# Stick-breaking attention: the clamp ahead of the softplus logarithm on GpSimd in place of VectorE

## The chip, the cores and the metric

The kernel runs on one core of one Trainium2 chip. The metric is the device time of one execution in microseconds; the time before is the median of three runs. An execution has five engines that run side by side, each through its own queue in order: TensorE (PE, with its weight loads as PEld), VectorE (DVE), ScalarE (ACT), GpSimd (POOL) and SyncE (SP), which only issues DMAs here.

## The reference

A trunk of two layers over 512 tokens of width 1024, all in float32: layer 0 mixes with an mLSTM, layer 1 with stick-breaking attention; after each mixer come a cross-attention into 256 memory tokens and a SwiGLU feed-forward of width 2816. The change lies in the mixer of layer 1, 16 heads of width 64:

```python
z = jnp.einsum('bhtd,bhsd->bhts', qb, kb) * scale
strict = s_idx < t_idx
log_1m = jnp.where(strict, jax.nn.log_sigmoid(-z), 0.0)
suffix = lax.cumsum(log_1m, axis=3, reverse=True) - log_1m
a = jnp.where(strict, jnp.exp(jax.nn.log_sigmoid(z) + suffix), 0.0)
outs.append(jnp.einsum('bhts,bhsd->bhtd', a, vb))
```

log_sigmoid(-z) is minus the softplus of z, so every score goes through one softplus, and the suffix sums and the final exponential follow from it.

## The kernel before

Every operation is first recorded in a plan, with an engine, a planned duration and the tiles that it reads and writes; `lay_out` then gives each engine its order by a list scheduling with due times (TensorE's recorded order sets the due times, tiles wait for free slots: 8 banks of PSUM, 44 "big" and 8 "half" buffers), and `emit` writes the instructions in the order of their planned starts. A planned duration that changes therefore moves other work. Some copies have an alternative engine: `copy` may go to ScalarE or, when VectorE is planned to be free earlier, to VectorE (L454 to L457).

Products are made from split operands (a high and a low part in float32r), three matmuls for one product. `split` (L546) makes the high part with a copy (L455 on ScalarE, L456 on VectorE) and the low part with a subtraction on VectorE (L470).

`stick` (L1216) works through 8 pairs of heads. For each pair `open_pair` (L1308) makes five banks of scores of 128x512 (zc, two zb, two za): matmuls of keys and queries (`scores`), closed by one matmul with the mask. Each bank goes through `softplus` (L1291): exp on ScalarE from the bank into a buffer s, the minimum with 1e13 on s, the logarithm of 1 + s on ScalarE, the maximum of z and s on VectorE, which reads the bank, and the split. Then `subtract` lets TensorE subtract the suffix sums from the same five banks, `weights` takes the exponentials, and the products with v follow. While a pair's softplus chains run, TensorE works on projections of the next pairs, on v, and on the keys of the cross-attention (`between`, the table STICK at L60).

So for each bank there is a stretch between its last score matmul and its first subtract matmul, which TensorE fills with a projection, and in which the five-step chain of softplus has to end. GpSimd's queue holds, in this stage, memsets of the key and query tiles (L503, two to a pair) and DMAs of the residual rows and the gains (L432). All five engines run in order, so that an instruction which waits holds back what is queued behind it on its engine.

Of the kernel before, what the change touches and what calls it, by code (L numbers as in the profile page):

```python
# [14 lines left out]
ALU = mybir.AluOpType  # L15
# [60 lines left out]
class View:  # L76
# [41 lines left out]
    def ap(self):  # L118
        r = self.buf.tile
        for s in self.steps:  # L120
            if isinstance(s, tuple):
                r = r[s]
            elif isinstance(s, int):
                r = r.rearrange("p (m n) -> p m n", n=s)
            elif s == "two":
                r = r.rearrange("p (a m) n -> p a m n", a=2)
            else:
                r = r.bitcast(s)
        return r
# [262 lines left out]
class Trunk:  # L392
# [823 lines left out]
    def stick(self, h, w_qkv, w_out, filler, finish):  # L1216
# [73 lines left out]

        def softplus(z, s, t):  # L1291
            self.act(s, z, AF.Exp)
            self.ts(s, s, 1e13, None, ALU.min)
            self.act(s, s, AF.Ln, bias=1.0)
            self.tt(s, z, s, ALU.max)
            self.split(t, s)
# [11 lines left out]
        def open_pair(qk):  # L1308

            zc, zb, za = self.bank(NT, P), {}, {}  # L1310
            scores(zc, zc[:, 0::2], [(e, 2, zc[:, 2 * e : 2 * e + 2]) for e in range(2)], qk)

            s, c = self.half(NT, P), Pair(self.big(6, P, dt=R), self.big(6, P, dt=R))
            softplus(zc, s, c[:, 0:4])
            sb, b = self.big(2, NT, P), Pair(self.big(2, NT, P, dt=R), self.big(2, NT, P, dt=R))
            for e in range(2):
                zb[e] = self.bank(NT, P)
                scores(zb[e], zb[e][:, 0::3], [(e, 1, zb[e][:, 0:3]), (e, 3, zb[e][:, 3:4])], qk)
                softplus(zb[e], sb[:, e], b[:, e])
            u = s[:, 1::2]  # L1320
            self.tt(u, u, sb[:, :, 3], ALU.add)
            self.split(c[:, 4:6], u)

            self.tt(sb[:, :, 1:3], sb[:, :, 1:3], s.pairs(), ALU.add)
            x = Pair(self.big(2, 3, P, dt=R), self.big(2, 3, P, dt=R))
            self.split(x, sb[:, :, 0:3])
            a = {}
            for e in range(2):
                za[e] = self.bank(NT, P)
                scores(za[e], za[e][:, 0], [(e, 0, za[e])], qk)  # L1330
                t = self.big(2, NT, P, dt=R)
                a[e] = Pair(t[:, 0], t[:, 1])
                softplus(za[e], self.half(NT, P), a[e])
            return zc, zb, za, c, b, a, x
# [410 lines left out]
```

## Time and profile before

| | us |
|---|---|
| median of three runs (1484.99 to 1488.79) | 1485.59 |
| the profiled execution, its own time | 1486.58 |
| span of its profile, first to last instruction | 1484.9 |
| TensorE busy | 1469.4 (99%) |
| VectorE busy | 1197.8 (81%) |
| ScalarE busy | 865.8 (58%) |
| GpSimd busy | 143.6 (10%) |
| the eight pairs of the stage with the change | from about 770 to 945 |

The mean granted clock of TensorE is 0.997 of its higher level. A busy share is a mean over all stages; the matmuls are pipelined and their ends are modelled, so that a matmul's duration is longer than the distance to the next one's start. Starts are therefore what to read of TensorE, and the same holds in a small measure for VectorE and ScalarE, where a row's start lies some 0.08 us ahead of the end of the row before it. Groups of rows are named by the line of the helper that recorded them (L470 is any two-operand VectorE operation, L475 any VectorE operation with scalars).

### The profile page before, as it was taken

To read this page: it belongs to the slowest core of one execution; us is meant where nothing else is said; L and a number is where in the kernel's file an instruction comes from. 1 tells how busy PE (TensorE), PEld (TensorE's weight loads), DVE (VectorE), ACT (ScalarE), POOL (GpSimd) and SP (SyncE) were. 2 spreads that over 40 slices of the span, in tenths; PEclk is the share of its full clock that TensorE was granted. 3 is DMA by queue.
4 is the path that set the end of the run, shared out by engine and by line. 5 is a ranking of instruction groups with operands and counts; after the bars stand their busy time and mean duration, and the time that the engine had idled before them with its cause. 6 is when DMAs were issued, how large, how long until landed. Compare 5 with 4: busy or idle time off the path is not lost.

```text
span 1484.9 us, 26101 instructions
## 1 busy us (share of the span) xinstructions
PE 1469.4 (99%) x10335; PEld 1370.6 (92%) x10335; DVE 1197.8 (81%) x1851; ACT 865.8 (58%) x1495; POOL 143.6 (10%) x179
## 2 busy tenths in 40 slices
PE   9999899999999999999999999999999999999998
PEld 7999889998999999998889889888988999999996
DVE  7988879887787877897838998878787968778985
ACT  7768656564654554544538997766546644444632
POOL 3100100100011111110100001001000111110100
PEclk9999999999999999999999999999999999999999
DMA  8445646532655575675343459255414563854741
GB/s 224 90 100 143 199 135 206 108 121 85 174 110 128 96 161 129 137 189 162 110 113 93 99 164 254 102 174 126 140 63 132 119 142 72 213 114 100 152 161 57
DMA packets 173228, 200.43 MB, mean 135 GB/s; under 512 B 8241, under 2 KB 142129, under 8 KB 173106
## 3 DMA queue, kind: packets, MB, share of 16 engines
q1 hardware_dynamic: 126192, 131.65, 28.8%
q0 software_dynamic: 46912, 67.12, 23.3%
q8 instruction: 81, 1.33, 0.4%
q14 instruction: 41, 0.34, 0.1%
q10 hardware_dynamic: 2, 0.00, 0.0%
HBM read 176.20 MB, written 10.49 MB: 126 GB/s over the span
## 4 chain that ended last, share of the span: by engine, by line
PE 94%; DMA 2%; DVE 2%; ACT 1%; issue 1%; DVEq 0%; POOL 0%; POOLq 0%; ACTq 0%
PE ps L526 92%; PE ps L540 2%; DMA big<-in_ffn_w_down_dram 1%; DVE big L470 1%; DMA big<-in_ml_w_in_dram 1%; ACT big L455 0%; DVE big L482 0%; ACT half L448 0%; DMA big<-in_norm_gains_dram 0%; DVE sm L475 0%; DVE half L470 0%; DVE sm L482 0%; ACT sm L448 0%; DVE big L456 0%; ACT half L455 0%
## 5 line engine op out<-in xcount | busy, mean ns | idle before, releaser
L526 PE MATMUL ps<-big,big 128*128 128x256 f32 (+2 forms) x9762 | 1407.4, 305 | 5.8 <-ACT big L455 2.8
L526 PEld LDWEIGHTS ps<-big,big 128*128 128x128 f32 (+1 forms) x9762 | 1298.0, 188 | 91.1 <-ACT big L455 3.3
L470 DVE TENSOR_TENSOR big<-big,big 128x1024 fp32r<-128x1024 f32 (+2 forms) x541 | 626.4, 1191 | 45.7 <-ACT big L455 25.1
L455 ACT CAST big<-big 128x1024 fp32r<-128x1024 f32 (+1 forms) x422 | 417.6, 1021 | 162.2 <-DMA big<-in_ffn_w_gate_up_dram 45.2
L470 DVE TENSOR_TENSOR big<-ps,big 128x512 fp32r<-128x512 f32 (+3 forms) x197 | 114.4, 605 | 44.2 <-ACT big L455 31.5
L455 ACT COPY half<-ps 128x512 f32<-128x512 f32 (+1 forms) x112 | 65.5, 585 | 124.1 <-PE ps L526 116.4
L455 ACT CAST big<-ps 128x512 fp32r<-128x512 f32 (+1 forms) x159 | 76.9, 513 | 99.6 <-PE ps L526 64.8
L448 ACT ACTIVATE half<-ps 128x512 f32<-128x512 f32 (+2 forms) x137 | 79.4, 581 | 90.2 <-PE ps L526 84.6
L448 ACT ACTIVATE half<-big 128x512 bf16<-128x512 f32 (+2 forms) x64 | 42.1, 659 | 73.0 <-DVE big L470 45.9
L437 POOL DMA_DIRECT2D big<-in_ffn_w_gate_up_dram x40 | 51.1, 1278 | 316.9 <-DVE big L470 217.4
L470 DVE TENSOR_TENSOR big<-half,big 128x512 fp32r<-128x512 f32 (+4 forms) x126 | 76.6, 625 | 5.9 <-ACT big L448 3.3
L482 DVE SCALAR_TENSOR_TENSOR half<-ps,half 128x512 f32<-128x512 f32 (+3 forms) x74 | 47.0, 645 | 36.4 <-PE ps L526 18.0
L455 ACT CAST big<-half 128x512 fp32r<-128x512 f32 (+3 forms) x82 | 43.9, 558 | 10.7 <-DVE half L470 6.3
L470 DVE TENSOR_TENSOR half<-ps,half 128x512 f32<-128x512 f32 (+1 forms) x54 | 36.4, 687 | 15.4 <-PE ps L526 11.9
L448 ACT ACTIVATE big<-ps 128x512 fp32r<-128x512 f32 (+2 forms) x66 | 39.6, 612 | 15.2 <-PE ps L526 11.8
L470 DVE TENSOR_TENSOR big<-ps,gain 128x512 f32<-128x512 f32 x32 | 22.0, 687 | 31.8 <-ACT half L448 30.0
L540 PE MATMUL ps<-const,big 128*128 128x128 f32 (+1 forms) x314 | 41.9, 270 | 0.8 <-DVE big L482 0.8
L540 PEld LDWEIGHTS ps<-const,big 128*128 128x128 f32 (+1 forms) x314 | 36.0, 140 | 6.0 <-DVE big L482 1.1
L475 DVE TENSOR_SCALAR sm<-sm,sm 128x1 f32<-128x1 f32 x101 | 24.2, 243 | 20.2 <-ACT half L448 11.4
L448 ACT ACTIVATE half<-half 128x512 f32<-128x512 f32 (+1 forms) x50 | 30.8, 630 | 10.3 <-DVE half L470 10.2
L482 DVE SCALAR_TENSOR_TENSOR big<-big,sm,gain 128x512 f32<-128x512 f32 (+1 forms) x45 | 34.9, 808 | 0.6
L482 DVE SCALAR_TENSOR_TENSOR big<-big,sm,big 128x512 f32<-128x512 f32 (+1 forms) x49 | 34.1, 737 | 0.8
(92 smaller groups left out, 588.2 us busy)
## 6 DMA issues: line engine op xcount, KB each, us to landing
big<-in_ffn_w_gate_up_dram SPq DMA_DIRECT2D x68, 512.0 KB, 5.0
big<-in_ffn_w_gate_up_dram POOLq DMA_DIRECT2D x40, 512.0 KB, 6.1
big<-in_ffn_w_down_dram SPq DMA_DIRECT2D x36, 512.0 KB, 5.9
big<-in_xa_w_kv_dram SPq DMA_DIRECT2D x32, 512.0 KB, 5.4
big<-in_sb_w_qkv_dram SPq DMA_DIRECT2D x24, 512.0 KB, 4.1
big<-big SPq DMA_DIRECT2D x80, 128.0 KB, 2.3
big<-in_ml_w_in_dram SPq DMA_DIRECT2D x18, 512.0 KB, 5.3
dr<-big POOLq DMA_DIRECT2D x16, 512.0 KB, 4.2
```

The lines of the kernel that those rows point to most:

```text
L437: "POOL", 1040, lambda nc: nc.gpsimd.dma_start(ap(out), ap(in_), accum_op=ALU.add), [in_, out], [out], load=ns
L448: nc.scalar.activation(ap(out), ap(in_), func, scale=ap(scale), **kw)
L455: "ACT", 0.833 * n + (60 if psum else 95), lambda nc: nc.scalar.copy(ap(out), ap(in_)), [in_], [out],
L470: self._dve(out, [a, b], lambda nc: getattr(nc, q).tensor_tensor(out=ap(out), in0=ap(a), in1=ap(b), op=op), eng)
L475: nc.vector.tensor_scalar(out=ap(out), in0=ap(a), scalar1=ap(s1), scalar2=ap(s2), op0=op0, **kw)
L482: lambda nc: nc.vector.scalar_tensor_tensor(out=ap(out), in0=ap(a), scalar=ap(s), in1=ap(b), op0=op0, op1=op1),
L526: nc.tensor.matmul(ap(out), lhsT=ap(a), rhs=ap(b), start=start, stop=stop, **kw)
L540: nc.tensor.transpose(ap(out), ap(in_), ap(ident))
```

## The change

One line of `softplus`. The minimum is recorded for GpSimd, with a planned duration of 700 ns, where `ts` recorded it for VectorE with 66 + 0.52 x 512 = 332 ns:

```diff
         def softplus(z, s, t):
             self.act(s, z, AF.Exp)
-            self.ts(s, s, 1e13, None, ALU.min)
+            self.plan.op("POOL", 700, lambda nc: nc.gpsimd.tensor_scalar(out=ap(s), in0=ap(s), scalar1=1e13, scalar2=None, op0=ALU.min), [s], [s])
             self.act(s, s, AF.Ln, bias=1.0)
             self.tt(s, z, s, ALU.max)
             self.split(t, s)
```

Forty instructions change their engine, five in each pair. Since the plan sees other durations, the orders of all engines change between the first and the last pair and are the same ahead of it and behind it. VectorE loses 40 instructions and takes 16 more copies than before (nine more casts of 128x1024 and seven more of 128x512, and one plain copy more against one cast of 128x256 less); ScalarE has 16 fewer. TensorE's instructions are the same in number and kind. In pairs 1 to 5 their order is the same too; in pairs 0, 6 and 7 the first subtract comes three matmuls earlier.

TensorE in pair 0, before: the end of the projection (the tile ps_8907, three matmuls to one product) and the first subtract, on the bank ps_8863. The numbers behind names are running numbers that differ between the two kernels.

```order
L526 MATMUL ps_8907<-big_8338,big_8707 128x512
L526 MATMUL ps_8907<-big_8373,big_8701 128x512
L526 MATMUL ps_8907<-big_8338,big_8701 128x512
L526 MATMUL ps_8863<-big_8930,const_459 128x512
L526 MATMUL ps_8863<-big_8919,const_459 128x512
L526 MATMUL ps_8863<-big_8939,const_459 128x2x128
L526 MATMUL ps_8863<-big_8932,const_459 128x2x128
L526 MATMUL ps_8969<-big_8316,big_8810 128x512
```

The same place after; the projection's tile is ps_8911 here:

```order
L526 MATMUL ps_8863<-big_8939,const_459 128x512
L526 MATMUL ps_8863<-big_8929,const_459 128x512
L526 MATMUL ps_8863<-big_8946,const_459 128x2x128
L526 MATMUL ps_8863<-big_8935,const_459 128x2x128
L526 MATMUL ps_8911<-big_8338,big_8707 128x512
L526 MATMUL ps_8911<-big_8373,big_8701 128x512
L526 MATMUL ps_8911<-big_8338,big_8701 128x512
L526 MATMUL ps_8970<-big_8316,big_8810 128x512
```

The last three matmuls of the projection stood ahead of the four subtracts and now stand behind them.

VectorE in pair 0, before, from the last evacuation of a projection to the first low part: the three minima, and the maxima of the first three banks.

```order
L482 SCALAR_TENSOR_TENSOR big_8869<-ps_8826,big_8869 128x512
L475 TENSOR_SCALAR half_8877<-half_8877 128x512
L475 TENSOR_SCALAR big_8889<-big_8889 128x512 x2
L470 TENSOR_TENSOR half_8877<-ps_8863,half_8877 128x512
L470 TENSOR_TENSOR big_8889<-ps_8871,big_8889 128x512
L470 TENSOR_TENSOR big_8889<-ps_8882,big_8889 128x512
L470 TENSOR_TENSOR big_8930<-half_8877,big_8919 128x512
L475 TENSOR_SCALAR half_8925<-half_8925 128x512
```

After:

```order
L482 SCALAR_TENSOR_TENSOR big_8869<-ps_8826,big_8869 128x512
L456 CAST big_8892<-big_8850 128x1024
L470 TENSOR_TENSOR big_8901<-big_8850,big_8892 128x1024
L470 TENSOR_TENSOR half_8877<-ps_8863,half_8877 128x512
L470 TENSOR_TENSOR big_8890<-ps_8871,big_8890 128x512
L470 TENSOR_TENSOR big_8890<-ps_8882,big_8890 128x512
L456 CAST big_8935<-big_8890 128x512
L470 TENSOR_TENSOR big_8939<-half_8877,big_8929 128x512
L470 TENSOR_TENSOR big_8946<-big_8890,big_8935 128x512 x2
```

The minima are gone; a split of a weight (the cast and the subtraction of 128x1024) stands in their place ahead of the maxima, and one cast of 128x512 that ScalarE made stands ahead of the low parts.

GpSimd in pair 7, after; before, these four DMAs of residual rows stood in a row with nothing between them:

```order
L1293 TENSOR_SCALAR half_10655<-half_10655 128x512
L1293 TENSOR_SCALAR big_10664<-big_10664 128x512
L432 DMA big_10685<-dr_8270 128x1024
L432 DMA big_10702<-dr_8364 128x1024
L1293 TENSOR_SCALAR big_10664<-big_10664 128x512
L1293 TENSOR_SCALAR half_10711<-half_10711 128x512
L432 DMA big_10737<-dr_8506 128x1024
L1293 TENSOR_SCALAR half_10739<-half_10739 128x512
L432 DMA big_10766<-dr_8565 128x1024
```

The minima of the third, fourth and fifth bank are queued behind DMAs.

## Rows read from the trace of the kernel before

**Rows 1.** The longest of TensorE's waits over the whole span, of six that the view lists (who waited for whom: us in total, times, longest us), and the stretch of the chain that ended last which covers the stage (start us, us, what).

```profile
PE ps L526 <- ACT big L455: 2.8, 1, 2.8
...
739.95 220.16 PE ps L526 x1222
```

**Rows 2.** Busy time by stretch, from 780 to 940 us (us; PE, PEld, DVE, ACT and POOL busy with counts, granted clock, DMA share, GB/s): one stretch of 20 us and the sum of the eight.

```profile
840.00:860.00 20.00, 20.00 (x104) 17.20 (x103) 18.56 (x31) 18.31 (x34) 3.44 (x6) 1.00 0.59 160
...
sum 160.00, PE 160.00 PEld 142.37 DVE 145.39 ACT 139.17 POOL 9.82; mean PE 20.00 PEld 17.80 DVE 18.17 ACT 17.40 POOL 1.23
```

**Rows 3.** The minima, by their line, from 760 to 945 us (durations min/median/max in ns), and one of VectorE's groups by shape from 780 to 940 us (count | busy us, mean ns | idle before).

```profile
L475 DVE TENSOR_SCALAR half<-half x24: 416/423/429, 772.8 to 932.8; 128x512 f32<-128x512 f32 x24
L475 DVE TENSOR_SCALAR big<-big x16: 415/428/553, 773.4 to 927.5; 128x512 f32<-128x512 f32 x16
...
L456 DVE CAST big<-big 128x1024 fp32r<-128x1024 f32 x1 | 0.7, 689 | 0.0
```

**Rows 4.** GpSimd's timeline near the start of the program: the four selects, which read and write their tile in place, as the minimum does (start us, us).

```profile
23.89 1.20 POOL L508 TENSOR_SCALAR_AFFINE_SELECT half<-half 128x512 f32<-128x512 f32 x1
25.00 0.68 POOL L508 TENSOR_SCALAR_AFFINE_SELECT half<-half 128x512 f32<-128x512 f32 x1
25.59 0.44 POOL L508 TENSOR_SCALAR_AFFINE_SELECT half<-half 128x256 f32<-128x256 f32 x1
25.95 1.66 POOL L508 TENSOR_SCALAR_AFFINE_SELECT half<-half 128x512 f32<-128x512 f32 x1
```

**Rows 5.** VectorE's timeline over the same time (start us, us).

```profile
21.75 0.16 DVE L482 SCALAR_TENSOR_TENSOR sm<-sm,sm 128x1 f32<-128x1 f32 x1
...
23.33 1.22 DVE L470 TENSOR_TENSOR big<-big,big 128x1024 fp32r<-128x1024 f32 x1
24.46 0.69 DVE L470 TENSOR_TENSOR big<-ps,big 128x512 fp32r<-128x512 f32 x1
25.07 0.63 DVE L482 SCALAR_TENSOR_TENSOR sm<-sm,sm 128x1 f32<-128x1 f32 x1
25.62 1.50 DVE L470 TENSOR_TENSOR big<-big,big 128x1024 fp32r<-128x1024 f32 x1
```

**Rows 6.** VectorE's timeline in pair 0 (start us, us, and in brackets the idle time before it and its releaser).

```profile
772.76 0.42 DVE L475 TENSOR_SCALAR half<-half 128x512 f32<-128x512 f32 x1
...
775.26 1.28 DVE L470 TENSOR_TENSOR big<-ps,big 128x512 f32<-128x512 f32 x2
776.45 0.68 DVE L470 TENSOR_TENSOR big<-half,big 128x512 fp32r<-128x512 f32 x1
777.05 0.42 DVE L475 TENSOR_SCALAR half<-half 128x512 f32<-128x512 f32 x1
777.39 0.69 DVE L470 TENSOR_TENSOR big<-big,big 128x512 fp32r<-128x512 f32 x1
...
778.66 0.69 DVE L470 TENSOR_TENSOR big<-big,big 128x512 fp32r<-128x512 f32 x1
```

**Rows 7.** TensorE's timeline in pairs 0, 6 and 7: the first subtract of the pair (four matmuls, big<-const as the matrix of the suffix sums is constant), and in pair 7 the filling projection ahead of it.

```profile
780.00 0.86 PE L526 MATMUL ps<-big,const 128*128 128x512 f32 x4
...
909.02 0.86 PE L526 MATMUL ps<-big,const 128*128 128x512 f32 x4
...
929.75 5.18 PE L526 MATMUL ps<-big,big 128*128 128x256 f32 x42
934.76 0.86 PE L526 MATMUL ps<-big,const 128*128 128x512 f32 x4
```

**Rows 8.** VectorE's timeline in pairs 6 and 7: in pair 6 the first minimum and the third bank's maximum, and in both the low parts that the first subtract needs last.

```profile
902.01 0.43 DVE L475 TENSOR_SCALAR half<-half 128x512 f32<-128x512 f32 x1
...
904.86 0.68 DVE L470 TENSOR_TENSOR big<-ps,big 128x512 f32<-128x512 f32 x1
...
907.67 0.69 DVE L470 TENSOR_TENSOR big<-big,big 128x512 fp32r<-128x512 f32 x1
...
933.18 1.29 DVE L470 TENSOR_TENSOR big<-big,big 128x512 fp32r<-128x512 f32 x2
```

**Rows 9.** Pair 3: ScalarE's exp of the second bank and its logarithms of the fourth and fifth, VectorE's low parts of the two zb banks, and VectorE's rows behind the subtracts, with their idle times.

```profile
835.29 0.60 ACT L448 ACTIVATE half<-ps 128x512 f32<-128x512 f32 x1
...
839.02 1.15 ACT L448 ACTIVATE half<-half 128x512 f32<-128x512 f32 x2
...
842.04 1.29 DVE L470 TENSOR_TENSOR big<-big,big 128x512 fp32r<-128x512 f32 x2
...
848.97 0.69 DVE L482 SCALAR_TENSOR_TENSOR big<-ps,big 128x512 fp32r<-128x512 f32 x1 [0.38 <-ACT big L448]
849.58 0.68 DVE L470 TENSOR_TENSOR big<-half,big 128x512 fp32r<-128x512 f32 x1
850.43 0.69 DVE L470 TENSOR_TENSOR big<-half,big 128x512 fp32r<-128x512 f32 x1 [0.18 <-ACT big L448]
851.41 0.69 DVE L470 TENSOR_TENSOR big<-half,big 128x512 fp32r<-128x512 f32 x1 [0.29 <-ACT big L448]
```

**Rows 10.** TensorE's timeline in pair 3: the filling projection, the first subtract, and the first product with v.

```profile
836.86 9.98 PE L526 MATMUL ps<-big,big 128*128 128x512 f32 x42
846.68 0.86 PE L526 MATMUL ps<-big,const 128*128 128x512 f32 x4
...
851.12 2.12 PE L526 MATMUL ps<-big,big 128*128 128x256 f32 x11
```

## The prediction

> **What bounds the kernel now.** I read first who ended the span. The chain of waits shows one single piece from 739.95 us on, 220.16 us of TensorE's matmuls, 1222 of them with no other engine between [rows 1]. The whole stage with the change (770 to 945 us) lies in it. Next the list of TensorE's waits: the longest of the six in the whole program is 2.8 us, and none lies in this stage, since the chain would show it [rows 1]. Matmul durations overlap, so I check by starts: the 42 filling matmuls of 128x512 in pair 3 take 846.68 - 836.86 = 9.82 us, 0.234 us each, with nothing lost between them [rows 10]. So TensorE is the bound, and it is fed without a gap. Taking work off VectorE can then gain nothing directly; the change can only cost, by delaying what TensorE takes up. How near that is, the stretches show: from 780 to 940 us VectorE is busy 145.39 of 160 us and ScalarE 139.17, GpSimd 9.82 [rows 2]. VectorE has 14.6 us of idle time, 9%.
>
> **What leaves VectorE.** Forty minima at a median of 423 to 428 ns [rows 3]. The next instruction starts 0.34 us after one (777.05 to 777.39) [rows 6], so VectorE is freed of 40 x 0.34 = 13.6 us, all beside busy matmuls: worth 0 on the path. The plan gives 16 copies to VectorE instead: nine of 128x1024, whose one example takes 689 ns [rows 3], less 0.08 us of overlap about 0.6 each, and seven of 128x512, of the minimum's size and duration, about 0.34: 5.4 + 2.4 = 7.8 us. ScalarE is freed of them; it was not the bound, 0 on the path. TensorE keeps all its matmuls, 0.
>
> **What a minimum costs on GpSimd.** The trace has none there. The nearest rows are the selects of 128x512 near the start, which also read and write one tile in place. They show 1.20, 0.68 and 1.66 us [rows 4], and the spread has a cause that VectorE's rows show [rows 5]. The first, from 23.89, ends at 25.10, 0.55 after a VectorE operation with two operands in SBUF has ended (23.33 + 1.22 = 24.55). The last ends at 27.61, 0.49 after such an operation (25.62 + 1.50 = 27.12). The second meets an operation with an operand in PSUM (24.46) and takes 0.68. In turn VectorE is held: a 128x1 operation that takes 0.16 us at 21.75 takes 0.63 at 25.07 and ends with the second select, and the subtraction at 25.62 takes 1.50 for 1.22, since the select of 128x256 ends at 26.03. So in this trace a GpSimd operation that reads SBUF and a VectorE operation with two SBUF operands go one after the other. I take 0.55 us for the minimum itself, with bounds of 0.49 and 1.66, plus the time for which it waits or makes VectorE wait.
>
> The Trainium skill has this rule and it speaks against the change (SBUF — State Buffer, Who interferes with whom): GpSimd has only the second port pair of VectorE, and one holder locks the other out for a whole instruction, also when VectorE merely reads two operands from SBUF. The rows at 25.07 and 25.62 agree. Without the rule the sum below would be 0; by it at its full length it becomes the first rival.
>
> **Pairs 1 to 5** keep TensorE's order, with 9.8 us of filler in pair 3. There VectorE writes the low parts for the first subtract until 842.04 + 1.29 = 843.33 [rows 9], and TensorE takes them at 846.68 [rows 10]: 3.35 us to spare. The four later minima, 2.2 us of GpSimd, run beside a cast, a subtraction of 128x1024 and a cast of 128x512, 0.6 + 1.2 + 0.34 = 2.1 us. One after the other from 835.89, the end of the second exp, they end at 840.2; the fifth logarithm now starts at about 839.5 (two in 1.15 from 839.02) [rows 9]. The chain is 0.7 us late, against 3.35, and behind the subtracts VectorE idles for 0.38, 0.18 and 0.29 us [rows 9], which takes the lateness up. Cost 0, at most 0.4 for each pair: 0 to 2.0.
>
> **Pair 0.** Three matmuls fewer stand ahead of the first subtract, so TensorE reaches it 3 x 0.234 = 0.70 us earlier, at 779.30 for 780.00 [rows 7]; the third matmul, the first that needs the last low part, at 779.77. That part now ends at 778.66 + 0.69 = 779.35 [rows 6]. The new order takes out two minima ahead of it and the sum of 128x256, and puts a cast in: 0.65 us less, 778.70, if nothing is held. That is 1.07 us to spare. Held one after the other: from 772.76 [rows 6], when the first minimum is ready, three minima, a cast and a subtraction of 128x1024 share VectorE's second operand, 3 x 0.55 + 0.6 + 1.2 = 3.45 us, to 776.2. The third logarithm follows (0.1 + 0.62), then the maximum (0.69): 777.6, where it now ends at 775.26 + 1.28 = 776.54. So 1.1 us late: 779.8. The fourth and fifth minimum may hold the three low parts for 0.55 each: 779.8 to 780.9 against 779.77. TensorE loses 0 to 1.1 us; I take 0.6.
>
> **Pair 6.** The same three matmuls are taken from ahead of the first subtract, so its third matmul comes at 909.02 + 0.46 - 0.70 = 908.78 [rows 7]. Ahead of the maxima stand only a cast and a subtraction of 128x512, so the shared time is 3 x 0.55 + 0.34 + 0.60 = 2.6 us from 902.01; the third maximum ends at about 906.0, for 905.54 now [rows 8], 0.5 late. The last low part, 907.67 + 0.69 = 908.36 now, is 0.65 earlier by the order: 908.2, and up to 1.1 more. Loss 0 to 0.5, taken 0.2.
>
> **Pair 7.** The three matmuls are of 128x256, (934.76 - 929.75) / 42 = 0.119 us each [rows 7]: the third subtract at 935.22 - 0.36 = 934.86. The low parts end at 933.18 + 1.29 = 934.47 [rows 8], 0.68 earlier without two minima, 933.8. Three minima are queued on GpSimd behind DMAs, and two of VectorE's subtractions of 128x1024 run beside the first ones. One of these can hold a minimum for 1.2 us, and each minimum a low part for 0.55: up to 2 us late, loss 0 to 1.0, taken 0.5. Behind such a minimum only DMAs wait, for rows that are wanted after the output projection: 0.
>
> **The sum.** 0.6 + 0.2 + 0.5 = 1.3 us, bounds 0 and 1.1 + 0.5 + 1.0 + 2.0 = 4.6. Against the profiled execution 1486.58 + 1.3 = 1487.9; that one lies 1.0 above the median of the three runs, so against the median 1485.59 + 1.3 = 1486.9.
>
> **Rivals.** *VectorE becomes the bound of the pairs by being held.* Each minimum holds VectorE for its full 0.55 us: 22.0 us, plus 7.8 of copies, less 13.6: 16.2 against 14.6 us of idle time. Per pair VectorE comes 5 x 0.55 = 2.75 us late to the rows behind the subtracts; idle time there gives back 0.85. The first product with v takes its operand at 851.12, which VectorE ends at 849.58 + 0.68 = 850.26 [rows 9, 10]: 0.86 to spare. So 1.0 us is lost in each of eight pairs, 8 us: 1493.9. It decides once a pair's lateness passes 1.7 us. For it: 9% of idle time is little, and more than half of VectorE's work here has two SBUF operands. Against it: the five maxima read PSUM, and much of a minimum can run beside them.
>
> *The minimum is slow on GpSimd in itself*, at the upper bound of 1.66 us. In pair 0 three take until 777.7, the third maximum ends at 779.2, and a cast and three low parts later it is 781.4 against 779.77: 1.6 lost, also in pairs 6 and 7. In pair 3 four take from 835.89 to 842.5, the fifth maximum is some 2.4 late, and behind 0.86 and 0.85 us of slack 0.7 is lost. 3 x 1.6 + 5 x 0.7 = 8.3, and 15 at 2 us for each: 1494 to 1501. For it only that no row shows this operation; against it the ends at 0.49 and 0.55.
>
> *Relief of VectorE pays*: for faster by 0.3%, 4.5 us would have to come out of TensorE's stage, which shows no wait. Something would have to shorten matmuls: 1481.
>
> **How the numbers follow.** About 0.3%, 4.5 us, is what a measurement of this kernel can tell from no change. Forecast, 1485.5 to 1490: 0.66. VectorE held: 0.23. Slow minimum: 0.08. Relief pays: 0.03. The forecast's bounds lie within 0.3% but for its last tenth; so faster 0.03, same 0.66, slower 0.31. The range takes in the forecast, a little below for the spread of the runs (1484.99 was seen), and the first rival with 1 us on top: 1484.8 to 1495.0; outside stay the slow minimum and the relief, 0.11, and the edges.
>
> **What would show it.** Right: forty rows of the changed line on GpSimd near 0.55 us, longer where a two-operand row of VectorE is under way, VectorE's low parts longer than 0.69 beside them; TensorE's order of time without a gap in pairs 1 to 5 and gaps of under 1.1 us ahead of the first subtracts of pairs 0, 6 and 7. The first rival: gaps ahead of the products with v in every pair. The second: rows of over 1.2 us on GpSimd with VectorE at its maxima. Wrong altogether: a gap of several us in one place, such as a minimum behind a DMA whose tile is not free.

## The result, and the profile after

The kernel after takes 1502.35 us (median of five runs, 1500.98 to 1503.06), the one before on the same chip 1485.52 (five runs, 1484.99 to 1488.79): the ratio is 1.0109, 95% interval 1.0095 to 1.0123. That is 16.8 us slower, where 1.3 were predicted, and outside the predicted range. The profiled execution took 1500.98 us and has a span of 1499.3 us, for 1486.58 and 1484.9 before.

The page of after begins with the busy times of the engines (us, share of the span, instructions); the row on the minimum is from its list of the costliest groups (count | busy us, mean ns | idle time of GpSimd before them).

```profile
PE 1474.5 (98%) x10335; PEld 1372.3 (92%) x10335; DVE 1198.3 (80%) x1827; ACT 857.0 (57%) x1479; POOL 208.3 (14%) x219
...
L1293 POOL TENSOR_SCALAR half<-half 128x512 f32<-128x512 f32 x24 | 37.9, 1579 | 96.4 <-ACT half L448 88.7
```

The view by source line shows the forty minima (durations min/median/max in ns), and who waited for them (us, times).

```profile
L1293 POOL TENSOR_SCALAR half<-half x24: 1479/1488/2030, 770.4 to 947.1; 128x512 f32<-128x512 f32 x24
L1293 POOL TENSOR_SCALAR big<-big x16: 1481/1488/2166, 772.2 to 943.3; 128x512 f32<-128x512 f32 x16
...
  ACT half L448: 14.6, 16
  ACT big L448: 10.3, 12
```

A minimum takes 1.49 us, three and a half times the 0.42 that it took on VectorE [rows 3], and up to 2.17 where something holds it. Five of them are needed for each pair.

TensorE's list of waits (us in total, times, longest us), of which the longest was one of 2.8 us ahead of the stage [rows 1], now begins with this:

```profile
PE ps L526 <- DVE big L470: 11.8, 17, 1.6
```

What is late there, the chain of waits shows in pair 1 (start us, us, what; the short pieces between them are left out).

```profile
794.45 0.60 ACT half L448
...
795.20 1.49 POOL half L1293
...
796.77 1.49 POOL big L1293
...
798.34 1.49 POOL big L1293
...
799.90 1.49 POOL half L1293
...
801.47 1.50 POOL half L1293
...
802.99 0.64 ACT half L448
...
803.65 0.57 DVE half L470
```

ScalarE's exponential releases the first minimum; from there the five stand one behind the other at a pitch of 1.57 us, the fifth logarithm follows at 802.99, the fifth maximum at 803.65, and the low parts behind them. VectorE's timeline over the same time shows what that does to its queue (start us, us, idle time before and its releaser):

```profile
798.96 0.69 DVE L470 TENSOR_TENSOR big<-ps,big 128x512 f32<-128x512 f32 x1
800.52 0.69 DVE L470 TENSOR_TENSOR big<-ps,big 128x512 f32<-128x512 f32 x1 [0.88 <-ACT big L448]
802.09 0.69 DVE L470 TENSOR_TENSOR half<-ps,half 128x512 f32<-128x512 f32 x1 [0.87 <-ACT half L448]
803.65 0.69 DVE L470 TENSOR_TENSOR half<-ps,half 128x512 f32<-128x512 f32 x1 [0.88 <-ACT half L448]
...
806.40 0.42 DVE L470 TENSOR_TENSOR big<-ps,big 128x256 fp32r<-128x256 f32 x1
```

VectorE waits some 0.87 us ahead of each of the last three maxima, and what is queued behind them waits too. The last row is such work: it evacuates a bank of the filling projection, whose matmuls of 128x256 then take the bank anew. TensorE's timeline shows who needs it, and the first subtracts of pairs 0 and 6, where [rows 7] have no wait:

```profile
778.56 0.73 PE L526 MATMUL ps<-big,const 128*128 128x512 f32 x2 [1.54 <-DVE big L470]
780.17 0.79 PE L526 MATMUL ps<-big,const 128*128 128x256 f32 x2 [0.89 <-DVE big L470]
...
806.87 2.03 PE L526 MATMUL ps<-big,big 128*128 128x256 f32 x15 [1.45 <-DVE big L470]
...
917.21 0.74 PE L526 MATMUL ps<-big,const 128*128 128x512 f32 x2 [0.75 <-DVE big L470]
918.83 0.51 PE L526 MATMUL ps<-big,const 128*128 128x256 f32 x2 [0.88 <-DVE big L470]
```

Behind the waits of pairs 0 and 6 TensorE's clock is at its lower level for a while, which the stretches show (us; busy times of PE, PEld, DVE, ACT, POOL; granted clock; DMA share; GB/s):

```profile
778.00:780.00 2.00, 0.73 (x2) 0.30 (x2) 2.00 (x3) 1.07 (x2) 1.92 (x2) 0.90 0.00 0
780.00:782.00 2.00, 1.82 (x5) 1.58 (x6) 1.97 (x5) 1.52 (x3) 1.49 (x3) 0.50 0.00 0
782.00:784.00 2.00, 2.00 (x8) 1.58 (x7) 2.00 (x4) 2.00 (x5) 0.00 (x0) 0.74 0.01 4
...
920.00:923.00 3.00, 3.00 (x14) 2.90 (x14) 3.00 (x6) 3.00 (x7) 0.29 (x1) 0.50 0.93 307
```

0.50 is 1.2 GHz for 2.4. Behind pair 0's waits TensorE loses some (0.10 + 0.50 + 0.26) x 2 = 1.7 us by it, behind pair 6's about as much (an estimate from these rows).

**Where the 16 us lie.** TensorE has the same matmuls in both kernels, so the start of the same matmul can be set side by side. Pair by pair the kernel after falls behind by 4.2, 1.7, 0.7, 1.6, 1.6, 0.5, 3.7 and 2.4 us, 16.4 in the stage; ahead of it there are two jumps, one near 680 us, together 2.4 us the other way, in a part where the two programs are the same; behind it the distance stays at 14.0 to 14.7 us, which is the distance of the two profiled executions. The eleven waits that the timeline shows in pairs 0 to 6 and the two of pair 7 come to 10.1 us, the lower clock to about 3.4. Of the rest, 2.9, some 2.1 is the first 0.2 us or so of each wait, which the modelled end of the matmul before it covers: from start to start the thirteen waits come to 12.2. About 0.8 stays open.

### The profile page after: what moved, and what is told of

The parts are those of the page before. It is cut to its first block, busy times and chain, and to the rows that moved or that the text cites. A ratio compares the mean times of both kernels' runs of the same rounds, so it can differ in the third digit from the quotient of the medians.

```text
span 1499.3 us, 26119 instructions
## 1 busy us (share of the span) xinstructions
PE 1474.5 (98%) x10335; PEld 1372.3 (92%) x10335; DVE 1198.3 (80%) x1827; ACT 857.0 (57%) x1479; POOL 208.3 (14%) x219
## 4 chain that ended last, share of the span: by engine, by line
PE 89%; DVE 3%; POOL 3%; ACT 3%; DMA 2%; issue 1%; SPq 0%; DVEq 0%; POOLq 0%; ACTq 0%
PE ps L526 86%; PE ps L540 2%; DVE big L470 2%; POOL half L1293 2%; ACT big L455 2%; DMA big<-in_ml_w_in_dram 1%; POOL big L1293 1%; ACT half L448 1%; DVE big L482 0%; DMA big<-big 0%; ACT big L448 0%; DVE half L470 0%; ACT half L455 0%; DVE big L456 0%; SPq L432 0%
## 5 line engine op out<-in xcount | busy, mean ns | idle before, releaser
L470 DVE TENSOR_TENSOR big<-big,big 128x1024 fp32r<-128x1024 f32 (+3 forms) x541 | 628.9, 1195 | 41.6 <-ACT big L455 20.8
L455 ACT CAST big<-big 128x1024 fp32r<-128x1024 f32 (+1 forms) x406 | 405.1, 1028 | 162.1 <-DMA big<-in_ffn_w_gate_up_dram 46.9
L1293 POOL TENSOR_SCALAR half<-half 128x512 f32<-128x512 f32 x24 | 37.9, 1579 | 96.4 <-ACT half L448 88.7
L526 PE MATMUL ps<-big,const 128*128 128x512 f32 (+2 forms) x160 | 35.7, 358 | 7.9 <-DVE big L470 7.9
L432 POOL DMA_DIRECT2D dr<-big x16 | 8.7, 544 | 240.3 <-DVE sm L475 213.5
```

Of the source, the lines that this page charges most:

```text
L432: self.plan.op(eng, cost, lambda nc: getattr(nc, q).dma_start(ap(out), ap(in_)), [in_, *behind], [out], load=ns)
L455: "ACT", 0.833 * n + (60 if psum else 95), lambda nc: nc.scalar.copy(ap(out), ap(in_)), [in_], [out],
L470: self._dve(out, [a, b], lambda nc: getattr(nc, q).tensor_tensor(out=ap(out), in0=ap(a), in1=ap(b), op=op), eng)
L526: nc.tensor.matmul(ap(out), lhsT=ap(a), rhs=ap(b), start=start, stop=stop, **kw)
L1293: self.plan.op("POOL", 700, lambda nc: nc.gpsimd.tensor_scalar(out=ap(s), in0=ap(s), scalar1=1e13, scalar2=None, op0=ALU.min), [s], [s])
```

## The experiments

**Order or duration?** The first kernel keeps the instruction order of after on every engine and cuts the minimum to 16 of the 512 columns; the second cuts it to 256. The rest of s is left unclamped.

```diff
-            self.plan.op("POOL", 700, ... out=ap(s), in0=ap(s) ..., [s], [s])
+            part = s[:, 0:1, 0:16]          # the second kernel: s[:, 0:2]
+            self.plan.op("POOL", 700, ... out=ap(part), in0=ap(part) ..., [s], [s])
```

> The order of every engine is that of the changed kernel, but each of the forty GpSimd minima covers 16 of the 512 columns (the other scores go unclamped). Length theory (a minimum takes 1.49 us on GpSimd, five stand in a row in each pair, and the softplus chains end too late for the first subtract) and hold theory (VectorE's operations with two operands in SBUF wait for GpSimd's reads): the cause is gone with the length, so 1485 to 1488 us. Order theory (the order that the plan laid out for 700 ns is worse in itself, with three matmuls less ahead of the first subtracts of pairs 0, 6 and 7): still 1498 to 1502.

Measured: 1486.7 us (ten runs) against 1485.62 of before on the same chip, ratio 1.0005 (0.9996 to 1.0015). No wait of TensorE is left in the stage, and its matmuls keep their distance to those of the kernel before to within 0.1 us from the first pair to the last. The durations:

```profile
L1294 POOL TENSOR_SCALAR half<-half x24: 237/247/1437, 772.9 to 932.0; 128x16 f32<-128x16 f32 x24
```

So the new order of all engines, the casts that went to VectorE and the three matmuls that moved cost nothing that this trace shows, and at most 2.2 us by the interval. The order by itself is not the cause.

> Same order again, each minimum over 256 of the 512 columns (the other half goes unclamped). If the 1.49 us go by columns, each takes about 0.75, near the planned 0.70. Length theory: the chains end when the plan meant them to, 1485.5 to 1489 us. Hold theory: half of the held time is left, so about half of the loss, 1492 to 1495. Order theory: 1498 to 1502.

Measured: 1489.05 us, ratio 1.0023 (1.0013 to 1.0032); one wait of TensorE in pair 0.

```profile
L1294 POOL TENSOR_SCALAR half<-half x24: 839/850/1722, 772.5 to 934.2; 128x256 f32<-128x256 f32 x24
```

With the same order the time goes from 1486.7 over 1489.05 to 1502.35 us as the median duration goes from 0.25 over 0.85 to 1.49. The loss isn't in proportion: 0.6 us more cost 2.4, the next 0.64 cost 13.3. That slack takes up most of the first step is the likely reason, not one that a run singles out.

**Lateness or held ports?** In the third kernel three memsets of s stand in place of each minimum: about the same time on GpSimd in the same order, but nothing is read. The attention then works on constants.

```diff
-            self.plan.op("POOL", 700, ... out=ap(s), in0=ap(s) ..., [s], [s])
+            def three(nc):
+                for _ in range(3):
+                    nc.gpsimd.memset(ap(s), 1.0)
+
+            self.plan.op("POOL", 700, three, [s], [s])
```

> Each minimum is replaced with three memsets of the same tile, which only write (the scores are lost, all of the attention works on constants); at about 0.45 us from one to the next they fill GpSimd for about as long as the minimum did, in the same place of the chain and the same order. Length theory: the loss stays, 1499 to 1503 us. Hold theory: VectorE isn't held by an operation that reads nothing, so the loss goes, 1486 to 1490.

Measured: 1505.4 us (four runs), ratio 1.0136 (1.0120 to 1.0152). Three memsets take 1.70 us from the start of the first to the end of the third (median), 0.2 more than a minimum. The memsets, and VectorE's subtractions of two SBUF operands beside them (count | busy us, mean ns | idle before):

```profile
L1295 POOL MEMSET half<- x72: 520/526/1104, 773.0 to 953.6; 128x512 f32 x72
```

```profile
L470 DVE TENSOR_TENSOR big<-big,big 128x1024 fp32r<-128x1024 f32 x14 | 17.0, 1221 | 0.2
...
L470 DVE TENSOR_TENSOR big<-big,big 128x512 fp32r<-128x512 f32 x20 | 13.1, 683 | 0.1
```

In the kernel before, over the same stretch (780 to 940 us):

```profile
L470 DVE TENSOR_TENSOR big<-big,big 128x1024 fp32r<-128x1024 f32 x18 | 21.6, 1219 | 0.0
...
L470 DVE TENSOR_TENSOR big<-big,big 128x512 fp32r<-128x512 f32 x20 | 13.2, 687 | 0.0
```

So VectorE isn't held here, and the loss is there in full and 3 us on top, with operations that are 0.2 us longer. In the kernel after the subtractions take longer, so VectorE is held there, but a loss of this size doesn't need it; what the hold adds in the kernel after, this run doesn't tell:

```profile
L470 DVE TENSOR_TENSOR big<-big,big 128x1024 fp32r<-128x1024 f32 x17 | 21.6, 1285 | 0.2
...
L470 DVE TENSOR_TENSOR big<-big,big 128x512 fp32r<-128x512 f32 x19 | 13.4, 729 | 0.1
```

**The plan's price.** The plan of after counts 700 ns for a minimum. This kernel gives it 1570, its pitch in pair 1, and lets the plan order everything anew.

```diff
-            self.plan.op("POOL", 700, ...
+            self.plan.op("POOL", 1570, ...
```

> The changed kernel with the minimum planned at 1570 ns, the distance from one to the next in its trace, so that the order is laid out for it: two matmuls of a filling projection of some 0.23 us more for each 0.5 us ahead of the first subtracts of pairs 0 and 6 (9.2 us of filler for 7.1). Length theory: most of the loss of pairs 0, 6 and 7 goes (some 10 of 16 us), that of pairs 1 to 5, whose TensorE order stays, remains: 1489 to 1495 us. Hold theory: the held time is the same, 1497 to 1503.

Measured: 1490.93 us (five runs), ratio 1.0036 (1.0023 to 1.0049). 16.8 us become 5.3: two thirds of the loss go when the order is made for the duration that the minimum has. In pair 0, 30 filling matmuls of 128x512 now stand ahead of the first subtract, where the order of after has 21:

```profile
772.22 7.16 PE L526 MATMUL ps<-big,big 128*128 128x512 f32 x30
...
780.61 0.51 PE L526 MATMUL ps<-big,const 128*128 128x256 f32 x2 [0.78 <-DVE big L470]
```

The wait of 2.43 us in that place shrinks to 0.78. One of the waits left is new (TensorE's list of waits, of the whole program):

```profile
PE ps L526 <- DVE big L470: 2.4, 5, 0.9
PE ps L526 <- DMA big<-big: 2.0, 1, 2.0
```

By TensorE's starts against the kernel before, 3.8 of the 6.0 us that this kernel loses in the stage lie at that one stop at 926.90 us, the wait and the lower clock behind it (0.72 from 925 to 930 us). The late softplus chains are left with some 2.

**Without a minimum.** The line is taken out; s is unclamped.

> No minimum at all (the scores go unclamped into the logarithm), laid out anew: what the relief of VectorE by 13.6 us is worth by itself. TensorE is the bound and waits for nothing in the stage, so 1484.5 to 1486.5 us; if relief of VectorE were worth something here, 1480 to 1483.

Measured: 1484.49 us (eleven runs) against 1486.75, ratio 0.9990 (0.9981 to 0.9998). That is all that the relief of VectorE is worth in the order that the plan makes for it, with no work on GpSimd either; in the stage itself TensorE's starts gain 0.2 us.

**The minimum beside the chain.** The kernel before keeps its minimum on VectorE and gets 80 more on GpSimd, of 128x192, which nothing waits for.

```diff
+            idle = self.scratch      # a tile of its own
...
+            def two(nc):
+                for c in (0, 48):
+                    nc.gpsimd.tensor_scalar(
+                        out=ap(idle), in0=ap(t.hi.bitcast(F32)[:, :, c : c + 48]), scalar1=1e13, scalar2=None, op0=ALU.min
+                    )
+
+            self.plan.op("POOL", 1, two, [t.hi], [idle])
```

> The kernel before, its minima on VectorE, with forty times two GpSimd minima of 128x192 beside it, about 0.7 us each, that read a high part after its copy and write a tile that nothing reads. TensorE's, VectorE's and ScalarE's orders are those of before except in pair 7. GpSimd then reads SBUF for as long as in the changed kernel, but no step of the softplus waits for it. Hold theory as the cause: VectorE loses up to 1.4 us for each, 1495 to 1510 us. Length theory: at most the slack is touched, 1485.5 to 1490.

Measured: 1491.99 us (four runs) against 1486.75, ratio 1.0041 (1.0027 to 1.0054). Neither theory had what the trace shows. VectorE is held: its subtractions of 128x512 (big<-big,big) take 784 ns on average in the stage, for 687 before. Yet TensorE runs level with the kernel before through pairs 0 to 4, its distance constant within 0.05 us. Of the 7.5 us that it loses in the stage 6.9 are lost in one place, in the wait and the lower clock behind it (0.56 from 875 to 880 us). VectorE's row, and the place:

```profile
L470 DVE TENSOR_TENSOR big<-big,big 128x512 fp32r<-128x512 f32 x20 | 15.2, 784 | 0.0
```

```profile
878.39 0.77 PE L526 MATMUL ps<-big,big 128*128 128x256 f32 x2 [4.80 <-DMA big<-big]
```

The matmul waits for the spreads, the DMAs from SBUF to SBUF that lay out keys and queries. The transfers of that stretch (DMA queue: packets, MB, share of 16 engines; then issues: count, KB each, median us from issue to landing):

```profile
q0 software_dynamic: 282, 1.04, 52.3%
q1 hardware_dynamic: 488, 0.76, 38.9%
...
gain<-in_norm_gains_dram POOLq DMA_DIRECT2D x2, 512.0 KB, 6.5
big<-big SPq DMA_DIRECT2D x5, 128.0 KB, 4.4
```

In the kernel before the same stretch (868 to 876 us) has no packet of q0:

```profile
q1 hardware_dynamic: 1402, 1.39, 73.7%
...
big<-big SPq DMA_DIRECT2D x6, 128.0 KB, 2.3
```

The two gain DMAs stand in GpSimd's queue. Before, they are issued at 855.81 us; here ten minima stand ahead of them, the first is issued at 869.47, and their packets meet the last of the eight spreads that SyncE issues from 863.68 on: the two issued behind the first gain land 6.2 and 7.9 us after their issue, the one ahead of them 2.4.

**Pairs 1 to 5 alone.** GpSimd forms the minimum in pairs 1 to 5, at the plan's price of 1570, VectorE in pairs 0, 6 and 7.

```diff
+            if self.on_pool:        # pairs 1 to 5
+                self.plan.op("POOL", 1570, ...
+            else:
+                self.ts(s, s, 1e13, None, ALU.min)
...
```

> The minimum on GpSimd in pairs 1 to 5 alone, planned at 1570 ns, on VectorE in pairs 0, 6 and 7; TensorE's order is that of before in every row. Length theory: pairs 1 to 5 have 11 to 14 us of filler, the chain is some 3 us longer and the work that VectorE holds for the filler is planned around it: 1486 to 1489 us, some 2 us under the kernel with all pairs planned at 1570. Hold theory: five eighths of the loss, 1495 to 1498.

Measured: 1491.12 us (five runs), ratio 1.0036 (1.0023 to 1.0049). Against before TensorE loses nothing in pairs 1 and 2, 0.4 and 0.6 us in pairs 3 and 4, and then 4.0 us around one stop that ends at 901.58: a wait of 2.21 us, for which the profile names no releaser, and the lower clock behind it. There the DMAs of GpSimd's queue lie among twelve spreads that SyncE issues from 886.22 on: the two gains, which are issued at 882.02 and 882.61 here, just ahead of them, and four DMAs of residual rows (issued at 891 to 896 us). The spreads land 7.1 us (median) behind their issue, and 4.1 in the kernel before from 886 to 904 us; the first two, issued ahead of the residual rows, already need 8.5. So the gains are late in this kernel too.

**Which operation is dear?** Five forms on 128x192, off the chain, eight of each.

```diff
...
+                if n == 0:
+                    g.tensor_scalar(out=ap(idle), in0=ap(src), scalar1=2.0, scalar2=None, op0=ALU.mult)
+                elif n == 1:
+                    g.tensor_copy(ap(idle), ap(src))
+                elif n == 2:
+                    g.tensor_tensor(out=ap(idle), in0=ap(src), in1=ap(src), op=ALU.add)
+                elif n == 3:
+                    g.tensor_scalar(... scalar1=1e13, scalar2=0.5, op0=ALU.min, op1=ALU.mult)
+                else:
+                    g.tensor_scalar(... scalar1=1e13, scalar2=None, op0=ALU.min)
```

> The kernel before with one GpSimd operation of 128x192 for each softplus beside it, off the chain, in five forms: a product with a constant, a copy, a sum of two operands, a minimum and a product in one, a minimum. By the two sizes measured (0.24 us for 16 columns, 0.84 for 256) the minimum takes about 0.68 us. If the price of 2.5 ns for a column belongs to the scalar form, the product takes the same 0.68 and the copy less (the select of 512 columns in the trace of before took 0.5 to 0.7, which would be 0.25 here); if it belongs to any read and write of float32, the copy takes 0.68 too. Time of the whole: 1485 to 1488 us.

Measured: 1495.43 us (one run), with the gain DMAs among the spreads again. The forms, in the order of the code:

```profile
L1305 POOL TENSOR_SCALAR const<-big x8: 693/699/713, 778.9 to 942.0; 128x192 f32<-128x192 f32 x8
...
L1307 POOL COPY const<-big x8: 343/364/730, 779.8 to 942.8; 128x192 f32<-128x192 f32 x8
...
L1309 POOL TENSOR_TENSOR const<-big x8: 757/826/869, 780.4 to 943.2; 128x192 f32<-128x192 f32 x8
```

A multiplication by a constant costs what the minimum cost in the kernel with 80 of them (median 687 ns for 192 columns), a copy half of it. So it is not the comparison that is dear. The sum of two operands, which has no scalar, takes 826 ns; it reads twice as much, so whether the scalar or any arithmetic makes the price stays open. The last two forms ran beside VectorE's two-operand work (medians of 1186 and 952 ns) and tell nothing of themselves.

**Are transfers alone enough?** The kernel before with a pause of memsets on GpSimd ahead of the gain DMAs of pair 4: 54, 38 and 42 of them. No minimum runs on GpSimd, and TensorE, VectorE, ScalarE and SyncE keep their order.

```diff
...
+        def late(nc):
+            for _ in range(54):             # 38, 42
+                nc.gpsimd.memset(ap(idle), 0.0)
+            return nc.gpsimd.dma_start(ap(g), ap(src))
+
+        self.plan.op("POOL", 1040, late, [src, *behind], [g], load=1400)
```

> The kernel before with 54 memsets of 128x192 on GpSimd (about 0.25 us each, some 14 us) right ahead of the first of the two gain DMAs of pair 4, and nothing else: no minimum on GpSimd, all orders on the other engines the same. The gain DMAs are issued at about 869 us in place of 855.81. Theory A (transfers collide): the 4096-byte packets of the gains fall among the spreads of keys and queries that SyncE issues from 863 to 873 us, the last spread lands about 4 us late, and TensorE stops once, for 3 to 5 us near 876 to 880 us, with its clock at the lower level behind it: 1490 to 1493 us. Theory B (GpSimd's minima did it by holding VectorE or by the load on SBUF): without minima there is no stall, 1485.5 to 1487 us.

Measured with 54: 1485.9 us (eleven runs) against 1485.92, ratio 0.9998 (0.9989 to 1.0007), no stop. But the pause was too long: the gains were issued at 874.38 us, behind all eight spreads. So it doesn't tell between the two theories; it shows that the memsets, and gains that are late without meeting the spreads, cost nothing.

> The kernel before with 38 memsets of 128x192 ahead of the first gain DMA of pair 4. With 54 a memset took 0.33 us in place of 0.25, so that the gains were issued at 874.4 us and their packets came from 877 us on, behind the spreads' 512-byte packets (875 to 877): that run could not tell. With 38 the gains are issued at about 869.1 us, between the second and fourth of the eight spreads, as in the kernel with the forms off the chain. Theory A (transfers collide): the gains' packets lie at 871 to 876 us, the spreads' last packets land late and TensorE stops once, for 3 to 5 us, in pair 5: 1490 to 1493 us. Theory B (minima needed): 1485.5 to 1487 us.

Measured with 38: 1490.68 us (ten runs) against 1486.45, ratio 1.0030 (1.0020 to 1.0039). The pause and the gain, SyncE's spreads, TensorE's stop, and the transfers from 868 to 876 us:

```profile
854.22 12.81 POOL L800 MEMSET const<- 128x192 f32 x38
866.98 0.54 POOL L801 DMA_DIRECT2D gain<-in_norm_gains_dram  x1
```

```profile
864.18 7.74 SPq L433 DMA_DIRECT2D big<-big  x8
```

```profile
875.42 0.76 PE L527 MATMUL ps<-big,big 128*128 128x384 f32 x4 [2.96 <-issue]
```

```profile
q1 hardware_dynamic: 913, 1.01, 51.2%
q0 software_dynamic: 288, 1.05, 49.4%
...
big<-big SPq DMA_DIRECT2D x6, 128.0 KB, 6.2
```

The view names no releaser of this stop ("issue"). The spread that is issued at 869.15 us is the one whose landing the trace lacks; the spreads issued ahead of it and behind it land at 874.8 and 875.8, and TensorE goes on between the two, at 875.42.

> The same with 42 memsets: the gains are issued at about 870.5 us, some 4 us behind the first of the eight spreads. Theory A: as with 38, a stall of 2 to 5 us in pair 5, 1489 to 1493 us. Theory B: 1485.5 to 1487 us.

Measured with 42: 1494.27 us (four runs), ratio 1.0049 (1.0032 to 1.0065), with a stop of 6.26 us at 882.25 in the profiled execution, which at 1498.48 us is the longest of the four. So the meeting of these transfers stops TensorE for 3 to 6 us, by nothing but 13 to 14 us of pause in GpSimd's queue. Spreads that land 2.3 us behind their issue need 6.2 with the gains among them.

**And back.** The kernel with 80 minima off the chain, less the ten of pair 4, so that the gains stand ahead again.

```diff
-            self.plan.op("POOL", 1, two, [t.hi], [idle])
...
+            if not 21 <= self.seen <= 25:       # the five banks of pair 4
+                self.plan.op("POOL", 1, two, [t.hi], [idle])
```

> The kernel with 80 minima of 128x192 off the chain, less the ten of pair 4, so that the gain DMAs stand where they stood before, ahead of the minima of pair 5. All other orders are those of the kernel with 80. Theory A (transfers collide): the single stall near 878 us and the lower clock behind it go, 1485.5 to 1487 us, although seventy minima still hold VectorE now and then. Theory B (minima hold VectorE): seven of eight pairs still pay, 1490 to 1492 us.

Measured: 1487.57 us (eleven runs) against 1485.92, ratio 1.0009 (1.0000 to 1.0017). The stop is gone, with seventy minima still beside VectorE. What they cost is 1.7 us by the medians, 2.5 at the end of the interval, and less by the trace: through pairs 0 to 6 TensorE keeps its distance to the kernel before within 0.05 us, and it loses 0.7 in pair 7, where its order differs.

## Why the prediction was wrong

**The step that failed is the price of the minimum.** The prediction took 0.55 us "for the minimum itself, with bounds of 0.49 and 1.66", from the selects [rows 4]. It measured 1.49. That lies within the bounds, but the sum was worked out with 0.55 alone, and the upper bound came in only as a rival outside the range. The selects were the nearest rows in that they work in place on the same shape, but they are another instruction. Three kernels show the price of this one: 0.25, 0.85 and 1.49 us at 16, 256 and 512 columns, (1.488 - 0.247) / 496 = 2.5 ns for a column; at 192 columns it is about twice a copy. The Trainium skill (GPSIMD Engine Reference, Engine selection) calls GpSimd roughly line-rate for operations with one input; against 0.42 us on VectorE the rows here say otherwise, and they decide. The first select's 1.20 and the last one's 1.66 were taken for 0.55 plus a hold, and that reading may stand; it said nothing of a minimum.

**What followed was the second rival**, "The minimum is slow on GpSimd in itself", which got 0.08. Its mechanism and its places came out: the three minima of pair 0 end at 775.8 us, in an execution that is 2.4 us ahead there, so at 778.2 for the rival's 777.7; the maxima and low parts follow late, pairs 0, 6 and 7 lose most, pairs 1 to 5 less. It gave 1494 to 1501 for 1.66 to 2 us; at 1.49 it was 1502.35, so it was priced too low as well. Two things were missing in it. TensorE's clock falls behind the waits of pairs 0 and 6: about 3.4 of the 16.4 us. And the rival counted only the operands of the subtracts. VectorE's queue is in order, so at each maximum that waits other work waits too, in pair 1 the evacuation that frees a bank for the filling projection.

**Pairs 1 to 5** were put at 0 to 2.0 us together, from 3.35 us of slack in pair 3 [rows 9, 10]. They lost 6.1. Four later minima at a pitch of 1.57 end 4 x 1.02 = 4.1 us later than at 0.55: more than the slack.

**The first rival**, VectorE held for the length of each minimum, got 0.23 and is wrong as the cause: the hold exists in the rows, but memsets that read nothing cost as much and more, and seventy minima of 128x192 beside the chain cost 1.7 us by the medians once the gains are back in place, none of it in pairs 0 to 6 by the trace. The rule that the Trainium skill states for it (SBUF — State Buffer, Who interferes with whom) agrees with VectorE's longer rows; it decides little here.

**Right were** the reading that TensorE bounds the stage without a wait, so that relief of VectorE is worth next to nothing (without any minimum 1484.49, ratio 0.9990), and that the new order by itself is free within the noise (1486.7 with 16 columns, ratio 1.0005).

**Nothing was expected of GpSimd's DMAs**: "Behind such a minimum only DMAs wait, for rows that are wanted after the output projection: 0". In the kernel after no wait for a DMA is shown, though the gains are issued at 890.96 us there for 855.81. But in five other kernels (80 minima off the chain, five forms, 38 and 42 memsets, and pairs 1 to 5 alone, there together with residual rows) the gains, issued later, met SyncE's spreads and TensorE stopped. With the plan's price put right the 5.3 us that remain hold a wait of 2.0 us for such a spread, beside 1.0 for late operands and the lower clock behind; that this one has the same cause is likely, since residual rows were issued at 909.56 us and the spreads near it needed 9.4 us to land, but only the gains were tried by themselves.

## What to carry to other kernels

Price an operation that is new to an engine by a row of the same instruction, and where there is none let the range reach to the far bound: for 128x512 the shortest select took 0.68 us [rows 4] and a memset 0.53, and neither tells of the minimum's 1.49. Where the duration enters a plan, a wrong number costs twice, by the work and by an order made for another duration; here the right number took back two thirds. An engine that seems idle may be free only because its DMAs are early: before work goes into its queue, ask which transfers stand behind it and what they will meet when they come later.

## What was unexpected

GpSimd's price for a minimum with a constant, 2.5 ns for a column of 128 float32 on top of 0.2 us, three and a half times VectorE's for 512 columns, and the same for a multiplication by a constant at 192. TensorE's clock, which fell to 0.50 in pair 0 behind waits of 1.54 and 0.89 us and stayed at 1.00 from 800 to 820 us although TensorE waited 1.45 us there. And 1 MB of gains from GpSimd's queue (q0), which took half of the 16 DMA engines for 8 us and made 128 KB transfers on the other queue land 6.2 us behind their issue for 2.3.
